# Value columns of two attention groups by seven block products, three units' weights prepared in the attention

## The chip, the cores and the metric

The kernel runs as one launch on one core of a Trainium2 chip. A core has engines that work side by side, each through its own instructions in their order: TensorE (PE, matrix products and, on a queue of its own, weight loads), VectorE (DVE), ScalarE (ACT), GpSimd (POOL) and SyncE (SP), which here starts nearly all transfers. They meet through semaphores. On-chip memory has 128 partitions; products are summed in 8 PSUM banks of 128 x 512 fp32. The metric is the device time of one execution in microseconds (us), lower is better.

## The reference, cut to what matters

The program is a two-layer decoder trunk over 1024 positions of width 1024 in fp32: layer 0 mixes positions with a chunked spatial gate, layer 1 is a dilated attention, each is followed by a squared-ReLU MLP of width 4096, and an RMS norm ends it. The change concerns the attention's products with `w_qkv`:

```python
qkv = (h @ w_qkv).astype(jnp.float32).reshape(B_, S_, 3, N_DIL_GROUPS, ATT_HEADS, HEAD_DIM)
...
for g, (window, dil) in enumerate(WINDOW_DILATIONS):
    n_, d_, m_ = _dilated_group(qkv[:, :, 0, g], qkv[:, :, 1, g], qkv[:, :, 2, g],
                                rb[:, g * ATT_HEADS:(g + 1) * ATT_HEADS], window, dil)
...
scales = [jnp.exp(m_ - m_all) for m_ in maxs]
num_sum = sum(n_ * c[..., None] for n_, c in zip(nums, scales))
den_sum = sum(d_ * c for d_, c in zip(dens, scales))
o = (num_sum / den_sum[..., None]).astype(h.dtype).reshape(B_, S_, ATT_WIDTH)
return o @ w_out
```

`h` here is normed. There are three groups of 8 heads of 64 columns with (window, dilation) = (128, 1), (512, 4), (2048, 16). In `_dilated_group` a query meets keys at the stride of its group, a bias from a table is added, and numerator, denominator and row maximum are returned. The values are 3 x 512 = 1536 columns, the queries and keys 3072.

## The kernel before, in words

**Products.** An fp32 operand is split into a rounded upper half and the rest (`split`: the copy to the upper half is on ACT at L219, the difference on DVE at L220). A product is three TensorE passes (upper x upper, upper x lower, lower x upper); one matmul instruction is a 128 x 128 weight against 128 x 512. Most large products also go by seven block products: two operands cut 2 x 2 need seven products of blocks and not eight, with sums of blocks formed before and of products after. All matmuls of this kind have line L191.

**Value stage** (`all_values`). The normed activations `y` lie in four blocks: half of the features x half of the positions. The 1536 value columns are three column groups `r` of 512. For each `r` and each half of the positions, 8 slices `k` of the features x 4 blocks of 128 positions x 3 passes are summed in four banks, directly and without block products: 96 matmuls. `firsts` holds the weights of column group 0; those of the next are loaded (`w_vt[r + 1, k]`, 256 KB each) and split in the second half of the current one, into the weight pool, which holds 8 pairs (tile name `wp`). Each finished bank is split into a tile `vs` and stored to `vd[r]` in DRAM.

Beside this run three generators. `terms_a.differences` forms, from the activations kept in fp32, the operands `t[4]` to `t[7]` of the block products for queries and keys; blocks 1 to 3 are `y` itself. `prepare` makes the seven weights of attention units 7, 8, 9 and 10: it loads four blocks of `w_qkv`, forms the sums on DVE, splits them (tiles `tr`) and stores both halves of each to `wd` in DRAM. `unit_weights`, advanced by `more()`, provides the weights of the units in their order: those of unit 0 are loaded, summed and split there, on POOL, the others are read back from `wd`, 512 KB each. Units 1 to 6 and 11 are prepared elsewhere, 11 by `prepare_apart`, which keeps the lower half in the tile that it loaded and puts the upper half in another, and hands the stores to `save`.

**Attention.** It has 12 units: 4 pairs of heads x 3 groups. `unit_qk` forms queries and keys of a unit by seven products (seven times 48 matmuls), reading `t[1]` to `t[7]` and the unit's weights. Other generators then form the scores (a DVE operation at L1401 adds the bias to the scores in PSUM and finds the maximum; ACT makes the exponentials at L1403), transpose them on TensorE (L198), split them (L219 and L220, tiles `tr`), multiply by the values `V`, which are loaded from `vd`, and merge the groups (tiles `N`; `od` in DRAM). A unit's bias is loaded (tile `t` from `bvec`) and copied by DVE, reversed, into a tile `b` at L1173 (`bias_turn`). The tag "b" of the pool `tpool` has two buffers, 128 x 512 each: the bias of unit i+1 goes into the one that unit i-1 leaves when its last scores are read.

**What sets the order.** TensorE's order is written by the program: a class `Flow` keeps a clock of estimated TensorE time, and the generators beside the main work yield a delay (the constants `PACE`, `LAT`, `CALM`, in ns) after which they are taken up again. On the other engines and in SP's queue the framework's scheduler orders the instructions by its own costs and priorities, and a pool's buffer is given again when its last reader has finished. SP starts the transfers in its order and waits there for what each needs.

## Time and profile before

| what | us |
|---|---|
| median of three runs (lowest to highest) | 2134.45 (2133.67 to 2135.84) |
| the profiled execution | 2131.01 |
| its span from first to last instruction | 2129.3 |
| one half (96 matmuls) of a value column group | 21.8 |
| unit 0 of the attention begins, from the span's start | 1059.6 |
| the attention's part that holds units 0 to 11, about | 1060 to 1396 |

One execution on the chip is recorded and shown as a page: the busy time of each engine, the same in 40 slices, the DMA queues, the chain of work that ended last (followed back from the end, at each step to what released it), the costliest groups of instructions and the DMA issues. The trace behind it answers closer questions: waits by what ended them, busy times by stretch of the span, a timeline. Times in rows are us, the mean of one instruction ns. A name as `wp<-r` is output and input tile, a line as L220 that of the code, where a helper's line stands for all that call it. "SPq" is SP's queue; a transfer's time is that from issue to landing.

### The profile page before, as it was taken

Reading aid. Unit: us, or ns where it says so; the run is one execution under the profiler, and the core shown is the slowest. Engines: PE = TensorE matmul, PEld = TensorE weight load, DVE = VectorE, ACT = ScalarE, POOL = GpSimd, SP = SyncE. Lnnn points to the kernel's source line nnn. Section 1 sums busy time; section 2 is a strip of 40 time slices with the busy share of each in tenths; the row PEclk is TensorE's granted clock in tenths of the full one; section 3 lists DMA queues with packets and bytes.
Section 4 is the critical chain, followed back from the end, with each engine's and each line's share of the span. In section 5 each row is a group of like instructions: output and inputs, shape, how many; then the busy total and the mean of one; then the engine's idle time right before and its main releaser. Section 6 shows DMA issues by size and latency. Waiting matters only on the chain.

```text
span 2129.3 us, 30657 instructions
## 1 busy us (share of the span) xinstructions
PE 2102.1 (99%) x10192; PEld 1739.0 (82%) x10192; DVE 1553.2 (73%) x2853; ACT 1170.5 (55%) x2360; POOL 511.1 (24%) x381
## 2 busy tenths in 40 slices
PE   9999999999999999999999999999999999999997
PEld 7888888888888888878888888887888888888886
DVE  7878769766789788688446666766985456987876
ACT  7645435566675444245356665766556556544432
POOL 2000224333324322420200000002343232433244
PEclk9999999999999999999999999999999999999999
DMA  6428814587756544449774656481256443654432
GB/s 218 125 92 287 289 59 139 202 284 270 265 195 201 163 144 139 139 173 323 267 231 148 182 157 177 164 275 61 74 200 210 152 155 125 207 163 153 149 114 79
DMA packets 221298, 380.79 MB, mean 179 GB/s; under 512 B 39513, under 2 KB 67284, under 8 KB 221140
## 3 DMA queue, kind: packets, MB, share of 16 engines
q1 hardware_dynamic: 212000, 377.48, 53.1%
q10 hardware_dynamic: 9140, 1.36, 0.4%
q8 instruction: 80, 1.31, 0.2%
q14 instruction: 78, 0.64, 0.1%
HBM read 245.94 MB, written 132.81 MB: 178 GB/s over the span
## 4 chain that ended last, share of the span: by engine, by line
PE 87%; DVE 6%; DMA 3%; ACT 1%; issue 1%; POOL 1%; SPq 0%; POOLq 0%; DVEq 0%; ACTq 0%
PE mm L191 44%; PE at L191 41%; PE at L198 2%; DVE y L220 1%; DVE t L220 1%; DVE wp L220 1%; DMA h<-in_xT 1%; DMA r<-in_w_v 0%; DVE r L437 0%; DMA t<-in_w_qkv 0%; DVE hx L220 0%; DMA V<-vd 0%; POOL t L277 0%; DVE h L332 0%; DVE b L442 0%
## 5 line engine op out<-in xcount | busy, mean ns | idle before, releaser
L219 ACT ACTIVATE wp<-r 128x512 fp32r<-128x512 f32 (+3 forms) x407 | 241.2, 597 | 352.1 <-PE at L191 217.2
L220 DVE TENSOR_TENSOR wp<-r,wp 128x512 fp32r<-128x512 f32 (+3 forms) x400 | 329.7, 829 | 132.8 <-ACT wp L219 130.0
L191 PE MATMUL mm<-t,wp 128*128 128x512 f32 x1368 | 345.4, 396 | 0.0
L191 PE MATMUL at<-hx,wp 128*128 128x512 f32 x1452 | 340.6, 389 | 1.5 <-DVE h L1043 1.5
L191 PEld LDWEIGHTS at<-hx,wp 128*128 128x128 f32 x1452 | 272.3, 188 | 59.1 <-DVE h L1043 2.4
L191 PEld LDWEIGHTS mm<-t,wp 128*128 128x128 f32 x1368 | 250.6, 188 | 52.6 <-issue 0.7
L277 POOL TENSOR_TENSOR t<-t 128x512 f32<-128x512 f32 (+1 forms) x64 | 82.2, 1284 | 686.5 <-ACT t L272 684.5
L191 PE MATMUL at<-y,wp 128*128 128x512 f32 x1008 | 245.3, 389 | 0.0
L191 PE MATMUL mm<-hx,wp 128*128 128x512 f32 x984 | 234.1, 389 | 0.0
L191 PEld LDWEIGHTS at<-y,wp 128*128 128x128 f32 x1008 | 189.1, 188 | 39.5 <-issue 0.3
L191 PEld LDWEIGHTS mm<-hx,wp 128*128 128x128 f32 x984 | 184.7, 188 | 38.3
L191 PE MATMUL mm<-y,wp 128*128 128x512 f32 x816 | 210.4, 397 | 1.2 <-DVE y L220 0.6
L375 POOL TENSOR_TENSOR t<-r 128x512 f32<-128x512 f32 (+3 forms) x62 | 82.9, 1336 | 480.2 <-DMA r<-in_w_up 136.9
L191 PEld LDWEIGHTS mm<-y,wp 128*128 128x128 f32 x816 | 149.1, 188 | 33.4 <-DVE y L220 1.0
L220 DVE TENSOR_TENSOR hx<-t,hx 128x512 fp32r<-128x512 f32 x192 | 162.6, 851 | 9.0 <-ACT hx L219 9.0
L191 PE MATMUL mm<-y,whi 128*128 128x512 f32 x512 | 158.2, 390 | 0.0
L219 ACT ACTIVATE hx<-t 128x512 fp32r<-128x512 f32 x192 | 119.1, 628 | 22.9 <-PE mm L191 10.0
L191 PE MATMUL at<-t,wp 128*128 128x512 f32 x552 | 130.6, 389 | 0.0
L377 POOL TENSOR_TENSOR r<-r 128x512 f32<-128x512 f32 (+3 forms) x62 | 91.0, 1468 | 163.5 <-DVE wp L220 156.5
L1043 DVE TENSOR_TENSOR h<-h,at 128x512 f32<-128x512 f32 x144 | 98.0, 681 | 34.9 <-PE at L191 34.2
L191 PEld LDWEIGHTS at<-t,wp 128*128 128x128 f32 x552 | 103.6, 188 | 21.5
L191 PEld LDWEIGHTS mm<-y,whi 128*128 128x128 f32 x512 | 95.6, 188 | 19.5
(228 smaller groups left out, 3452.4 us busy)
## 6 DMA issues: line engine op xcount, KB each, us to landing
t<-hid SPq DMA_DIRECT2D x182, 256.0 KB, 4.1
wd<-tr SPq DMA_DIRECT2D x154, 256.0 KB, 3.1
wp<-wd SPq DMA_DIRECT2D x77, 512.0 KB, 3.9
hid<-t SPq DMA_DIRECT2D x140, 256.0 KB, 2.9
r<-in_w_up SPq DMA_DIRECT2D x120, 256.0 KB, 2.8
r<-in_w_dn SPq DMA_DIRECT2D x80, 256.0 KB, 2.6
hid<-b SPq DMA_DIRECT2D x56, 256.0 KB, 2.9
r<-in_w_v SPq DMA_DIRECT2D x48, 256.0 KB, 3.1
```

The lines of the kernel that those rows point to most:

```text
L191: nc.tensor.matmul(out, lhsT, rhs, **kw)
L198: nc.tensor.transpose(out, src, ident)
L219: nc.scalar.activation(hi, src, AF.Copy)
L220: (engine or nc.vector).tensor_tensor(lo, src, hi.bitcast(F32), op=ALU.subtract)
L277: nc.gpsimd.tensor_tensor(self.acc, self.acc, sq, op=ALU.add)
L375: tt(r3, r[0, 0], r[1, 0], op=ALU.subtract)
L377: tt(r[1, 1], r[1, 0], r[0, 0], op=ALU.subtract)
L1043: return engine.tensor_tensor(hs[i, s], hs[i, s], src, op=ALU.add).ins
```

## The change

The value columns of group 0 stay as they are. Those of groups 1 and 2 together are now one 2 x 2 block product: features in two halves, and the two column groups. `VSEQ` is the order of the seven products; each takes 4 slices x 4 blocks x 3 passes for each of four position blocks at a time, 48 matmuls. The activation operands are the `t` that queries and keys use. The weight operands are made by `value_operands` as they are needed: it fetches `EARLY` operands ahead (32 loads of 256 KB for both groups, where there were 16), forms sums on DVE, 16 in all, and splits 28. Four banks `sums` collect products 1, 6, 7, 4, four others product 2 and then 5, 3. Tiles `uk` keep the copies (by ACT) that later sums need, and `added` makes the sum on DVE that `value_store` splits and stores. `differences` now forms its operands in the order in which these products need them.

With it the weights of the units move. Unit 7 is made in the value stage from product 6 on, by `prepare_apart`. Units 8, 9 and 10 are made in the attention: a generator is added there with a first delay of 12,000 and a `PACE` of 7,000 ns a step. Their loaded tiles `ra` have four buffers of the tag "r"; their upper halves `hi` lie in the tag "b", the two buffers of the bias tiles. Each unit has seven pairs: 21 `hi` in all, each split on ACT and DVE and stored with its `ra`. Unit 0's weights are formed on DVE and not on POOL. The bias of unit 0 is loaded in the value stage.

```diff
-PREPARED = ((1, 2, 3, 4, 5, 6), (7, 8, 9, 10))
+PREPARED = ((1, 2, 3, 4, 5, 6), (7,), (8, 9, 10))
 APART = 11
-PACE = (1700.0, 2500.0, 1900.0)
+EARLY = 4
+PACE = (1700.0, 1800.0, 3000.0, 7000.0)
...
         def differences(self, pace):
 
             tt = nc.vector.tensor_tensor
-            for k in range(4):
-                yield self.there[k], 0
-                (y00, y10), (y01, y11) = ((t[k][:, 0, :], t[k][:, 1, :]) for t in (self.kept, self.more))
-                for p, out, a, b in ((5, y00, y01, y00), (7, y01, y11, y01), (6, y11, y11, y00), (4, y10, y10, y11)):
-                    tt(out, a, b, op=ALU.subtract)
-                    self.t[p].append(pair(f"t{p}").split(out))
-                    yield pace
+            parts = [[t[k][:, j, :] for t in (self.kept, self.more) for j in range(2)] for k in range(4)]
+            for y00, y10, y01, y11 in parts:
+                tt(y00, y01, y00, op=ALU.subtract)
+                self.t[5].append(pair("t5").split(y00))
+                yield pace
+            for y00, y10, y01, y11 in parts:
+                tt(y01, y11, y01, op=ALU.subtract)
+                tt(y11, y11, y00, op=ALU.subtract)
+                self.t[6].append(pair("t6").split(y11))
+                yield pace
+                tt(y10, y10, y11, op=ALU.subtract)
+                self.t[7].append(pair("t7").split(y01))
+                yield pace
+            for y00, y10, y01, y11 in parts:
+                self.t[4].append(pair("t4").split(y10))
+                yield pace
...
-    def fetch(src):
-        r = rtemp()
+    def fetch(src, own=rtemp):
+        r = own()
         return r, load(src, r.bitcast(F32))
+
+    def apart():
+        return tpool.tile([P, HALF], F32R, tag="r", name="ra", bufs=4)
+
+    def above():
+        return tpool.tile([P, HALF], F32R, tag="b", name="hi", bufs=2)
...
-    def placed(dst, held):
+    def placed(dst, held, own=rtemp):
         lo, r = held
-        hi = rtemp()
+        hi = own()
         split(hi, lo, r)
         unsaved.extend((dst[:, e, :], t) for e, t in enumerate((hi, lo)))
...
-    def prepare_apart(i):
+    def prepare_apart(i, own=rtemp, upper=rtemp):
 
         tt = nc.vector.tensor_tensor
         n = 3 * (i // 3 * 3 + ORDER[i % 3])
         src = lambda a, b: w_qkv[n + a][:, half(b)]
-        put = lambda p, held: placed(wd[i, p], held)
-        r10, r11 = fetch(src(1, 0)), fetch(src(1, 1))
+        get = lambda a, b: fetch(src(a, b), own)
+        put = lambda p, held: placed(wd[i, p], held, upper)
+        r10, r11 = get(1, 0), get(1, 1)
...
+    def attended(unit_list, pace, *own):
+        for i in unit_list:
+            for _ in prepare_apart(i, *own):
+                yield pace
+                save()
+        save()
...
     def unit_weights():
 
-        tt = nc.gpsimd.tensor_tensor
+        tt = nc.vector.tensor_tensor
         for i, w in enumerate(unit_w):
...
             def put(p, src):
-                w[p] = wpair().split(src, nc.gpsimd)
+                w[p] = wpair().split(src)
...
+    def value_store(r, b, src):
+        v = slot((P, 4, 4, 64), F32R, "vs")
+        p4 = src.rearrange("p (u a c) -> p u a c", u=4, a=2)
+        hi, lo = v[:, :, 0:4:3, :], v[:, :, 1:3, :]
+        nc.scalar.activation(hi, p4, AF.Copy)
+        nc.vector.tensor_tensor(lo, p4, hi.bitcast(F32), op=ALU.subtract)
+        nc.sync.dma_start(vd[r][blk(b)], v.bitcast(F32))
+
+    VSEQ = (1, 2, 5, 6, 7, 3, 4)
+
+    def value_operands():
+        tt = nc.vector.tensor_tensor
+        parts = {1: ((1, 0),), 2: ((1, 4),), 5: ((2, 0), (2, 4)), 6: ((1, 0),), 7: ((2, 4),), 3: ((1, 4),), 4: ((2, 4),)}
+        order = [(p, k) for p in VSEQ for k in range(4)]
+        fetched = lambda p, k: [load(w_vt[a, b + k], raw() if p == 5 and not b else temp()) for a, b in parts[p]]
+        total, held = {}, [fetched(*x) for x in order[:EARLY]]
+        for n, (p, k) in enumerate(order):
+            r = held.pop(0)
+            if n + EARLY < len(order):
+                held.append(fetched(*order[n + EARLY]))
+            x = r[0]
+            if p == 5:
+                tt(x, r[0], r[1], op=ALU.add)
+                total[k] = x
+            elif p == 6:
+                x = total[k]
+                tt(x, x, r[0], op=ALU.subtract)
+            elif p in (7, 3):
+                tt(x, x, total[k], op=ALU.subtract)
+            yield wpair().split(x)
+
     def all_values():
 
...
+        operands, wv = value_operands(), []
+        for s in range(2):
+            ks = range(KT) if s == 0 else [4 * j + k for k in range(4) for j in range(2)]
+            banks = [mm_bank() if s == 0 and x < 3 else at_bank() for x in range(4)]
+            for n, k in enumerate(ks):
+                y = terms_a.blocks[k // 4, s]
+                flow.until(lambda: len(y) > k % 4)
                 for b, bank in enumerate(banks):
...
+                    x, w, c = y[k % 4], firsts[k], blk(b)
+                    matmul(bank, x.hi[:, c], w.hi, start=(k == 0), stop=False)
+                    matmul(bank, x.hi[:, c], w.lo, start=False, stop=False)
+                    matmul(bank, x.lo[:, c], w.hi, start=False, stop=(k == KT - 1))
+                    flow.pump()
+                if s:
+                    wv.append(next(operands))
+            for b, bank in enumerate(banks):
+                value_store(0, 4 * s + b, bank)
+        flow.add(terms_a.differences(PACE[1]))
+
+        uk = [slot((P, 2, HALF), F32, "uk") for _ in range(4)]
+
+        def added(x, bank):
+            t = temp()
+            nc.vector.tensor_tensor(t, x, bank, op=ALU.add)
+            return t
+
+        sums = None
+        for n, p in enumerate(VSEQ):
+            if p == 1:
+                sums = banks = [at_bank() for _ in range(4)]
+            elif p in (2, 5):
+                others = banks = [mm_bank() if b < 3 else at_bank() for b in range(4)]
+            else:
+                banks = others if p == 3 else sums
+            if p == 6:
+                flow.add(attended(PREPARED[1], PACE[2]))
+            opens = p in (1, 2, 5)
+            w = [wv.pop(0) for _ in range(4)]
+            x = terms_a.t[p]
+            for b, bank in enumerate(banks):
+                u, k1 = uk[b][:, 0, :], uk[b][:, 1, :]
+                for k in range(4):
+                    flow.until(lambda: len(x) > k)
+                    c, last = blk(b), k == 3
+                    matmul(bank, x[k].hi[:, c], w[k].hi, start=k == 0 and opens, stop=False, skip_group_check=True)
+                    matmul(bank, x[k].hi[:, c], w[k].lo, start=False, stop=False, skip_group_check=True)
+                    matmul(bank, x[k].lo[:, c], w[k].hi, start=False, stop=last, skip_group_check=True)
+                    flow.pump()
+                if p in (1, 6):
+                    nc.scalar.activation(u, bank, AF.Copy)
+                elif p == 2:
+                    value_store(1, b, added(u, bank))
+                elif p == 5:
+                    nc.scalar.activation(k1, bank, AF.Copy)
+                elif p == 7:
+                    value_store(2, 4 + b, added(k1, bank))
+                elif p == 3:
+                    value_store(1, 4 + b, added(u, bank))
+                else:
+                    value_store(2, b, bank)
+                if 0 < n < 6:
+                    wv.append(next(operands))
+                elif n == 6 and b:
+                    more()
+            if n == 5:
+                for _ in range(4):
+                    more()
+                U[0].rev = bias_tile(U[0].hp, U[0].g)
...
         if i == 0:
-            u.bias = bias_turn(*bias_tile(u.hp, g))
+            u.bias = bias_turn(*u.rev)
...
     all_values()
     for gen in (scorer, turner, valuer):
         flow.add(gen())
+    flow.add(attended(PREPARED[2], PACE[3], apart, above), 12000.0)
     for i in range(NU):
```

Where instructions stand now. On TensorE before, from the end of group 0's first half over its second half (the last 96 of the 99) into group 1, whose first half goes on as the last rows do (`wp` a weight pair, `y` a block of activations, `mm` and `at` banks of the two pools):

```order
L191 MATMUL mm<-wp,y 128x512 x9
L191 MATMUL at<-wp,y 128x512 x99
L191 MATMUL mm<-wp,y 128x512 x9
L191 MATMUL at<-wp,y 128x512 x3
L191 MATMUL mm<-wp,y 128x512 x9
```

The same place after (lines have moved by one): the second half of group 0 and product 1 (48 more), product 2 (48), then product 5 with the first four operands of `differences`:

```order
L192 MATMUL mm<-wp,y 128x512 x9
L192 MATMUL at<-wp,y 128x512 x147
L192 MATMUL mm<-wp,y 128x512 x36
L192 MATMUL at<-wp,y 128x512 x12
L192 MATMUL mm<-wp,t_9417 128x512 x3
L192 MATMUL mm<-wp,t_9430 128x512 x3
L192 MATMUL mm<-wp,t_9444 128x512 x3
L192 MATMUL mm<-wp,t_9458 128x512 x3
```

TensorE's order is 48 matmuls shorter. From unit 0 on it has the same shapes in both.

DVE before, from the bias copy for unit 4 to the row ahead of unit 4's first score read, an operation at L1401 (`N` the merge, `tr` transposed tiles, `q` and `k` lower halves of queries and keys, `st` a row's maxima):

```order
L1173 COPY b<-t 128x512
L1590 TENSOR_TENSOR N<-N,t 128x512
L1442 TENSOR_TENSOR N<-N,at 64x256
L1332 TENSOR_TENSOR t<-t,mm 128x512
L1442 TENSOR_TENSOR N<-N,at 64x256
L220 TENSOR_TENSOR tr<-at,tr 128x384
L1327 SCALAR_TENSOR_TENSOR q_11622<-t,q_11621 128x32x16
L220 TENSOR_TENSOR tr<-at,tr 128x384
L220 TENSOR_TENSOR tr<-N,tr 128x512
L1327 SCALAR_TENSOR_TENSOR k_11714<-mm,k_11713 128x32x16
L1442 TENSOR_TENSOR N<-N,at 64x256 x2
L220 TENSOR_TENSOR tr<-at,tr 128x384 x2
```

The same place after (the copy is now L1197, a split's difference L221, a score read L1494):

```order
L221 TENSOR_TENSOR ra<-ra,hi 128x512
L221 TENSOR_TENSOR tr<-at,tr 128x384
L221 TENSOR_TENSOR tr<-N,tr 128x512
L1420 SCALAR_TENSOR_TENSOR k_11724<-mm,k_11723 128x32x16
L221 TENSOR_TENSOR ra<-ra,hi 128x512
L1535 TENSOR_TENSOR N<-N,at 64x256 x2
L221 TENSOR_TENSOR ra<-ra,hi 128x512
L221 TENSOR_TENSOR tr<-at,tr 128x384 x2
L584 TENSOR_TENSOR ra<-ra 128x512
L1197 COPY b<-t 128x512
L1494 ISA t,st_11869<-at,b 128x128
L1494 ISA st_11869 128x1
```

The bias copy now stands directly ahead of the first scores that follow, behind splits whose `hi` use the buffer that the copy takes. Ahead of it in the whole gap stand four such splits; in the six gaps before units 2 to 7 there are three, four, three, four, three and four.

SP's queue at that place after (`wp<-wd` are weights of the coming units, `wd<-hi` and `wd<-ra` the stores of the new pairs, `ra<-in_w_qkv` their loads):

```order
L1390 DMA V<-vd_9037 64x4x256
L556 DMA wd_7_170<-hi 128x512
L556 DMA wd_7_170<-ra 128x512
L1241 DMA wp<-wd_4_146 128x1024
L556 DMA wd_3_173<-hi 128x512
L181 DMA ra<-in_w_qkv 128x512
L556 DMA wd_3_173<-ra 128x512
L1697 DMA od_1_11781<-tr 128x512
L556 DMA wd_6_171<-hi 128x512
```

The stores and loads of units 8 to 10, which stood in the value stage, are now among the attention's own transfers.

More of the change, by code (lines that the diff above doesn't have):

```diff
@@ L1246, in more @@
             next(ending, None)
-    def all_values():
-        ws, wn = firsts, []
-        for r in range(3):
-            if r == 1:
-                flow.add(prepare(PREPARED[1], PACE[2]))
-            for s in range(2):
-                ks = range(KT) if s == 0 else [4 * j + k for k in range(4) for j in range(2)]
-                banks = [mm_bank() if s == 0 and x < 3 else at_bank() for x in range(4)]
-                for n, k in enumerate(ks):
-                    y = terms_a.blocks[k // 4, s]
-                    flow.until(lambda: len(y) > k % 4)
-                    for b, bank in enumerate(banks):
-                        x, w, c = y[k % 4], ws[k], blk(b)
-                        matmul(bank, x.hi[:, c], w.hi, start=(k == 0), stop=False)
-                        matmul(bank, x.hi[:, c], w.lo, start=False, stop=False)
-                        matmul(bank, x.lo[:, c], w.hi, start=False, stop=(k == KT - 1))
-                        flow.pump()
-                    if s and r < 2:
-                        wn.append((k, wpair().split(load(w_vt[r + 1, k]))))
-                    elif s and n < AHEAD:
-                        more()
-                for b, bank in enumerate(banks):
-                    v = slot((P, 4, 4, 64), F32R, "vs")
-                    p4 = bank.rearrange("p (u a c) -> p u a c", u=4, a=2)
-                    hi, lo = v[:, :, 0:4:3, :], v[:, :, 1:3, :]
-                    nc.scalar.activation(hi, p4, AF.Copy)
-                    nc.vector.tensor_tensor(lo, p4, hi.bitcast(F32), op=ALU.subtract)
-                    nc.sync.dma_start(vd[r][blk(4 * s + b)], v.bitcast(F32))
-            if r == 0:
-                flow.add(terms_a.differences(PACE[1]))
-            ws, wn = dict(wn), []
```

10 lines of the change are left out of this document (5 added, 5 removed).

## The prediction

> **What bounds the kernel now.** I read the page's busy times first, then the chain that ended last, then TensorE's own waits, then busy times by stretch of the span, and last the timeline of the places that the change touches.
>
> ```profile
> span 2129.3 us, 30657 instructions
> PE 2102.1 (99%) x10192; PEld 1739.0 (82%) x10192; DVE 1553.2 (73%) x2853; ACT 1170.5 (55%) x2360; POOL 511.1 (24%) x381
> PE 87%; DVE 6%; DMA 3%; ACT 1%; issue 1%; POOL 1%; SPq 0%; POOLq 0%; DVEq 0%; ACTq 0%
> ```
>
> TensorE (PE) is busy for 99% of the span and makes up 87% of the chain. Its waits from the end of the value columns to the end of attention are these, as total, number and longest:
>
> ```profile
> PE at L191 <- DVE t L1574: 1.9, 3, 0.6
> PE mm L191 <- ACT o L219: 1.9, 1, 1.9
> PE mm L191 <- DVE h L332: 0.8, 1, 0.8
> PE at L191 <- DMA V<-vd: 0.7, 1, 0.7
> PE mm L191 <- DVE o L220: 0.2, 1, 0.2
> ```
>
> That is 5.5 us in 420. By stretches (all of the value stage but the first half of group 0; then attention):
>
> ```profile
> core 0: us, PE busy (x) PEld busy (x) DVE busy (x) ACT busy (x) POOL busy (x), PEclk, DMA share, GB/s
> 950.00:1060.00 110.00, 110.00 (x487) 91.13 (x486) 70.26 (x112) 49.07 (x87) 12.21 (x10) 1.00 0.81 295
> 1060.00:1396.00 336.00, 334.09 (x2081) 275.68 (x2079) 216.50 (x681) 213.49 (x590) 1.77 (x2) 1.00 0.59 176
> ```
>
> In the value stage PE never pauses, so a matmul less there is time saved, until another engine is late. VectorE (DVE) has 40 us free there. In attention PE pauses for 2 us in 336, and DVE and ScalarE (ACT) are busy for 64%.
>
> **What goes: 48 matmuls.** Groups 1 and 2 took 2 groups x 2 halves x 8 k x 4 blocks x 3 passes = 384; seven products take 7 x 4 x 4 x 3 = 336.
>
> ```profile
> 993.66 22.44 PE at L191 x99
> ```
>
> This piece of the chain gives 22.44 / 99 = 0.2267 us for one. 48 x 0.2267 = 10.9 us, all on PE. PE's order behind unit 0's start is the same, so nothing else of PE moves.
>
> **What the value stage gets.** Prices:
>
> ```profile
> L220 DVE TENSOR_TENSOR wp<-r,wp 128x512 fp32r<-128x512 f32 x8 | 5.5, 689 | 2.3 <-ACT wp L219 2.3
> L219 ACT ACTIVATE wp<-r 128x512 fp32r<-128x512 f32 x8 | 5.1, 632 | 5.5 <-PE at L191 5.3
> L220 POOL TENSOR_TENSOR wp<-r,wp 128x512 fp32r<-128x512 f32 x6 | 7.6, 1298 | 112.5 <-DMA vd<-vs 111.7 <-ACT wp L219 0.7
> r<-in_w_vt SPq DMA_DIRECT2D x8, 256.0 KB, 3.6
> ```
>
> DVE gains 51 operations in all: 12 more splits of value weights (28, not 16), 16 to form them, 12 sums with a kept product, and 11 of unit 0's weights that POOL did at 1.3 us each. It loses the 33 of units 8 to 10, which go to attention. In DVE's order 134 operations stand between the first stores of group 0 and unit 0's first q, where 115 stood. The 115 took the 70.26 us above, 0.61 each; 134 take 82 us, and PE's time there is 98. So DVE has room, if in order it is nowhere held up. The operand of a product can be split only when the product two before has released its weight buffer; walking the order with 0.61 us an operation, the tightest is the fourth operand of product 6, ready nearly 4 us ahead of PE. ACT gains 12 splits and 12 copies, loses 21 splits, and has 61 us free. The queue loses units 8 to 10 (18 loads and 42 stores of 256 KB) and gains 16 loads. I take 0 for the stage. Its bounds: not below 0, since PE waits for nothing there; above, one operand late by one load, 3.6 us.
>
> **What attention gets.** Units 8 to 10 bring 21 splits, 12 sums on DVE, 18 loads and 42 stores. As bare work, 33 x 0.61 = 20 us of DVE and 21 x 0.63 = 13 us of ACT go into some 190 us that have about a third free: nothing. What counts is where the upper halves lie: in the two buffers that hold the units' bias tiles. One is free only from the last score read of unit i-1 until the bias of unit i+1 is copied in. The order puts three or four upper halves into that gap in turn, six times (3, 4, 3, 4, 3, 4 for 21), and each has to be stored before the next is written. The copy waits for the last store, and behind it in DVE's order stand the score reads of unit i. The gap before unit 4 (four turns) now:
>
> ```profile
> 1196.03 0.42 DVE L1401 CUSTOM_DVE_ANT_0 t<-at,b 128x256 f32<-128x256 f32 x1
> 1198.06 0.42 DVE L1173 COPY b<-t 128x512 f32<-128x512 f32 x1
> 1205.98 1.02 DVE L220 TENSOR_TENSOR tr<-at,tr 128x384 fp32r<-128x384 f32 x2
> 1207.31 0.29 DVE L1401 CUSTOM_DVE_ANT_0 t<-at,b 128x128 f32<-128x128 f32 x1 [0.31 <-PE at L191]
> 1207.69 0.40 ACT L1403 ACTIVATE t<-t,st 128x128 f32<-128x128 f32 x1 [1.36 <-issue]
> 1208.87 0.39 ACT L1403 ACTIVATE t<-t,st 128x128 f32<-128x128 f32 x1
> 1211.08 1.03 PE L191 MATMUL at<-tr,V 128*128 128x256 f32 x8
> 1214.07 0.60 PE L198 MATMUL at<-ident,t 128*128 128x128 f32 x4
> ```
>
> The last read ends at 1196.45, and the copy, 1.6 us later, has 9 us to spare. The first read of unit 4 is at 1207.31, its exponentials end at 1209.26, and PE transposes them at 1214.07: 4.8 us in hand. The gap before unit 1 (three turns):
>
> ```profile
> 1100.95 0.08 DVE L1401 DVE_READ_ACCUMULATOR2_ANT st<- 128x1 f32 x1
> 1113.35 0.29 DVE L1401 CUSTOM_DVE_ANT_0 t<-at,b 128x128 f32<-128x128 f32 x1 [0.79 <-PE at L191]
> 1117.26 0.39 ACT L1403 ACTIVATE t<-t,st 128x128 f32<-128x128 f32 x1
> 1120.13 0.60 PE L198 MATMUL at<-ident,t 128*128 128x128 f32 x4
> ```
>
> 12.3 us, and 2.5 in hand at its eighth read. A turn is a split (0.63), two handovers (0.1 each, as from the read's end at 1207.60 to the exponential at 1207.69) and the store's landing. Landings, first attention, last the value stage:
>
> ```profile
> od<-tr SPq DMA_DIRECT2D x9, 256.0 KB, 2.9
> wp<-wd SPq DMA_DIRECT2D x67, 512.0 KB, 3.7
> V<-vd SPq DMA_DIRECT2D x12, 512.0 KB, 4.8
> wd<-tr SPq DMA_DIRECT2D x42, 256.0 KB, 3.3
> ```
>
> The nearest by size is 2.9, but the 60 added transfers are 15.7 MB in 190 us, 83 GB/s on 176, which takes the share from 0.59 to about 0.87 by its own ratio. That is the value stage's load, so I take 3.3: a turn is 4.13. Four turns, the copy (0.42) and the 1.95 from first read to last exponential: 16.5 + 2.4 = 18.9, so 1215.3 where PE needs 1214.07, 1.3 us late. Three times that is 4 us. Three turns with the copy take 12.8 for 12.3, inside the 2.5 in hand: 0. The ends: at 2.9 no passage costs anything; at 4.8 a four-turn one costs 7.3 and a three-turn one about 2.5, 29 us in all.
>
> By a rule of the Trainium skill (DMA: Bandwidth & Descriptors, on the anatomy of one DMA) a transfer takes 2.0 us and its bytes at 436 GB/s, an estimate of 2.6 us for 256 KB; by that the passages would cost nothing and the sum would be the first rival's. The same page (Latency and other measured facts) says that memory latency grows from 0.2 to 2 us under high load, which speaks against this change. The rows here, 2.9 at a share of 0.59 and 3.3 at 0.81, go that way.
>
> **The sum.** 2131.01 (profiled execution) - 10.9 + 0 + 4 = 2124.1. It stands 3.4 us under the median of the runs, so 2127.5 on their scale, 0.33% under 2134.45.
>
> **Rivals.**
> - *The whole saving stays* (landing about 2.9, or PE's slack is larger): 2134.45 - 10.9 = 2123.5. For it speaks the row of 256 KB stores in attention; against it the added load, and the order in which ACT does a split only behind other work.
> - *The passages eat most of the saving.* At 3.7, as 512 KB loads take, a turn is 4.53 and a four-turn passage 2.9 late, 8.6 in all: 2132.2, within 0.2%.
> - *VectorE holds the value stage.* If the operands of three products come late by one load each, 10.8 us go: 2138.3, also within 0.2%. Against it: 16 us free.
> - *Slower: the bias buffer decides.* At 4.3, between the loads' 3.7 and 4.8, a turn is 5.13: four turns 5.3 late, three turns 1 late, 19 us in all: 2142.5. It turns to slower by 0.2% where the stores land in 4.1 or more. For it speaks that V loads and weight loads stand just ahead of the stores in the one queue, which now waits for PE in front of them; a store behind such a wait lands later still:
>
> ```profile
> SPq L1217 <- PE mm L191: 167.5, 53, 5.4
> ```
>
> Against it: walking the six places, the load ahead of each first store is released in time. PE's waits would then pass 3 us. By the Trainium skill (TensorE: Matmul & The Clock Gate, Part 1) an idle window of some 3.4 us halves PE's clock, which would add to this rival; no run here shows it, with a clock of 1.00 in both stretches and no wait over 1.9.
>
> **Chances.** Forecast (2125.5 to 2130) 0.36; whole saving 0.22; passages at 3.7 0.13; VectorE 0.09; slower 0.20. A measurement of this kernel can tell about 0.2%, 4.3 us, from no change. Faster 0.58, same 0.22, slower 0.20. The range runs from 2122.5, the whole saving and 1 us of scatter, to 2141, which leaves out most of the slower case. The faster cases alone lie in 2123 to 2130.
>
> **What will show it.** The page should count 48 matmuls fewer (10144), and unit 0 should start about 98 us behind the second half of group 0, with no PE wait in between; a wait there for DVE or ACT at the weights means the third rival. DVE's count rises by 51. In attention I expect waits of 1 to 2 us before units 2, 4 and 6 for transposed tiles or exponentials, stores of the upper halves landing in about 3.3, and the bias copy idle on such a store. No waits there means the whole saving; waits of 5 us at all six places, the slower case. The prediction is wrong if the queue is blocked in attention so that weights of a unit come late, which I have at nothing.

## The result and the profile after

The changed kernel takes 2151.86 us (median of 6 runs, 2149.22 to 2156.07), the kernel before 2134.41 (6 runs). The ratio is 1.0081, with a 95% interval of 1.0068 to 1.0094: slower by 17 us, where 7 us less were forecast. The profiled execution has a span of 2149.0 us. Its page, in the lines that were shown of before:

```profile
span 2149.0 us, 30646 instructions
PE 2103.0 (98%) x10144; PEld 1736.4 (81%) x10144; DVE 1575.6 (73%) x2904; ACT 1183.9 (55%) x2384; POOL 498.0 (23%) x370
PE 79%; DVE 8%; DMA 6%; ACT 3%; issue 2%; POOL 1%; SPq 1%; ACTq 0%; DVEq 0%; POOLq 0%
```

TensorE has the 48 matmuls less, and yet its busy time is 0.9 us longer: the others took 11.8 us more. Its share of the chain fell from 87% to 79%, and DVE, DMA and ACT took what it lost. By stretches (the value stage from the same matmul as in the rows of before; then the attention), the longest of TensorE's waits from unit 0 on, and the chain in the value stage:

```profile
941.00:1051.00 110.00, 110.00 (x487) 91.10 (x486) 91.68 (x149) 57.39 (x100) 0.00 (x0) 1.00 0.58 210
1051.00:1410.00 359.00, 342.90 (x2072) 280.47 (x2070) 234.48 (x711) 222.95 (x607) 0.00 (x0) 0.98 0.66 205
```

```profile
PE at L192 <- DVE N L1535: 7.4, 5, 2.5
PE at L192 <- DVE tr L221: 3.6, 5, 1.7
PE at L192 <- DMA V<-vd: 2.6, 1, 2.6
```

```profile
1004.93 24.48 PE at L192 x108
1029.41 8.16 PE mm L192 x36
1037.57 13.60 PE at L192 x60
1051.17 8.84 PE mm L192 x39
```

The value stage runs without a pause, at 24.48 / 108 = 0.2267 us a matmul, and unit 0 starts at 1051.17 where it was 1059.6. In the attention TensorE is idle for 16 us of 359. As its order has the same shapes from unit 0 on, the two executions can be laid over each other matmul by matmul from the end. The shift of after against before is +2.4 us ahead of the value stage (waits at the program's start that change from execution to execution), -8.5 at unit 0 (so the stage gave 10.9), +15.8 from 1290 us of before on, when units 8 to 10 are made (24.3 lost in between), +19.4 behind the wait for `V` (3.6 more), and +19.7 at the end.

What happens in such a place, ACT and DVE ahead of unit 4's scores, then TensorE; the brackets give the idle time ahead and what ended it:

```profile
1209.02 0.63 ACT L220 ACTIVATE hi<-ra 128x512 fp32r<-128x512 f32 x1 [3.43 <-DMA wd<-hi]
1211.71 0.63 ACT L220 ACTIVATE hi<-ra 128x512 fp32r<-128x512 f32 x1 [0.61 <-DMA wd<-hi]
1218.08 0.40 ACT L1496 ACTIVATE t<-t,st 128x128 f32<-128x128 f32 x1 [4.97 <-DVE st L1494]
1217.41 0.43 DVE L1197 COPY b<-t 128x512 f32<-128x512 f32 x1 [2.25 <-DMA wd<-hi]
1213.71 0.88 PE L192 MATMUL at<-k,q 64*128 64x128 f32 x11 [1.70 <-DVE tr L221]
```

ACT stands at the third of the four upper halves (1209.02) until the second is stored, the bias copy stands behind the last store, and the first exponential comes at 1218.08. The chain of waits goes through three of the stores there (start, us); of its nine such pieces from 1090 to 1290 us four are longer than 5 us:

```profile
1203.78 5.16 DMA wd<-hi
1209.67 1.96 DMA wd<-hi
1212.37 4.96 DMA wd<-hi
```

### The profile page after: what moved, and what is told of

It reads as the page before. It is cut to its first block, busy times and chain, and to the rows that moved or that the text cites. A ratio compares the mean times of both kernels' runs of the same rounds, so it can differ in the third digit from the quotient of the medians.

```text
span 2149.0 us, 30646 instructions
## 1 busy us (share of the span) xinstructions
PE 2103.0 (98%) x10144; PEld 1736.4 (81%) x10144; DVE 1575.6 (73%) x2904; ACT 1183.9 (55%) x2384; POOL 498.0 (23%) x370
## 4 chain that ended last, share of the span: by engine, by line
PE 79%; DVE 8%; DMA 6%; ACT 3%; issue 2%; POOL 1%; SPq 1%; ACTq 0%; DVEq 0%; POOLq 0%
PE at L192 40%; PE mm L192 39%; DMA wd<-hi 2%; PE at L199 1%; DMA t<-in_w_qkv 1%; DVE tr L221 1%; DVE t L221 1%; DVE y L221 1%; POOL t L278 1%; DMA r<-in_w_v 1%; ACT t L1496 1%; DVE wp L221 1%; DMA V<-vd 0%; DVE r L438 0%; DVE h L333 0%
## 5 line engine op out<-in xcount | busy, mean ns | idle before, releaser
L221 DVE TENSOR_TENSOR wp<-r,wp 128x512 fp32r<-128x512 f32 (+3 forms) x399 | 322.8, 814 | 138.9 <-ACT wp L220 136.5
L220 ACT ACTIVATE wp<-r 128x512 fp32r<-128x512 f32 (+3 forms) x399 | 236.0, 596 | 328.4 <-PE at L192 202.5
L221 DVE TENSOR_TENSOR hx<-t,hx 128x512 fp32r<-128x512 f32 x192 | 162.1, 849 | 7.9 <-ACT hx L220 7.9
```

The lines of the kernel that those rows point to most:

```text
L220: nc.scalar.activation(hi, src, AF.Copy)
L221: (engine or nc.vector).tensor_tensor(lo, src, hi.bitcast(F32), op=ALU.subtract)
```

## The experiments

Times are medians of the same call's runs; the ratios are to the kernel before. "us" worked out from a ratio is that of 2134.4. Lines of code have moved with some edits, so that a helper has another number. A difference of two ratios carries about 0.2%, 4 us; one of 0.1% can't be told from nothing.

| run | median us | ratio, 95% interval |
|---|---|---|
| products, units 8 to 10 not made (none_made) | 2125.16 | 0.9958, 0.9943 to 0.9973 |
| units 8 to 10 moved, values direct (move_only) | 2158.82 | 1.0112, 1.0095 to 1.0129 |
| units 7 to 10 made in the value stage (in_value) | 2153.25 | 1.0088, 1.0073 to 1.0103 |
| upper halves in one own buffer (own_one) | 2152.67 | 1.0085, 1.007 to 1.01 |
| upper halves in tag t (among_t) | 2154.61 | 1.0106, 1.0086 to 1.0125 |
| lower half stored twice (unheld) | 2157.86 | 1.0109, 1.0094 to 1.0124 |
| their stores from ACT's queue (act_queue) | 2170.04 | 1.0167, 1.0149 to 1.0185 |
| 9500 ns a step (pace95) | 2150.98 | 1.0074, 1.0058 to 1.009 |
| operations alone (work_only) | 2142.07 | 1.0038, 1.0023 to 1.0052 |
| transfers alone (moves_only) | 2134.75 | 0.9995, 0.9985 to 1.0004 |
| operations alone, unit 8 only (work_one) | 2127.46 | 0.9967, 0.9955 to 0.9979 |
| operations alone, DVE's part on GpSimd (work_pool) | 2149.65 | 1.0062, 1.0043 to 1.008 |
| all, DVE's part on GpSimd (all_pool) | 2164.85 | 1.0138, 1.0118 to 1.0159 |
| ACT's operations alone (act_only) | 2127.57 | 0.9969, 0.9957 to 0.998 |
| DVE's operations alone (dve_only) | 2132.33 | 0.9991, 0.9983 to 1.0 |
| operations alone, upper halves in tag t (work_t) | 2128.23 | 0.9975, 0.9966 to 0.9984 |
| units 8 to 10 beside the first layer's down products (in_down) | 2128.61 | 0.9968, 0.9957 to 0.9979 |
| the same beside its up products (in_up) | 2175.07 | 1.0191, 1.0176 to 1.0206 |

**Which half of the change costs.** Theory A is the prediction's own: the bias buffers.

```diff
     # before, with the generators of after
+    flow.add(attended(PREPARED[2], PACE[3], apart, above), 12000.0)
```

> The kernel before with units 8 to 10 made in the attention as in the changed kernel (same tiles, same first delay and pace); the value columns stay direct. Theory A (each upper half holds a bias buffer until its store has landed; ACT, DVE and then TensorE stand behind it): the full loss of the attention, 24 us and up to 28 with the late V load: 2158 to 2163. Rival B (the 60 transfers and 54 operations cost by themselves, whatever buffer they use): the same here, told apart by the next two. Rival C (the block products cost in a place that is not in the value stage, by later V loads): nothing here, 2132 to 2139.

```diff
-    flow.add(attended(PREPARED[2], PACE[3], apart, above), 12000.0)
...
-                    nc.sync.dma_start(t.bitcast(F32), wd[i, p])
+                    nc.sync.dma_start(t.bitcast(F32), wd[i - 3 if i in PREPARED[2] else i, p])
```

> The changed kernel without the making of units 8 to 10: these units read the weights of units 5 to 7 again, so the same transfers come in for their weights, but 18 loads, 21 splits, 12 sums and 42 stores are left out, and the output is another. A and B: the products' saving alone, 2134.4 - 10.9 = 2123.5, with up to 2 us for a late V load. C: no saving, 2134 or more.

The move alone costs 24 us, the products alone gain 0.42%, 9 us. So the loss lies in making units 8 to 10 in the attention: 0.81% + 0.42% = 1.23%, 26 us. Theory C falls but for a rest: the last wait for `V` is there in none_made too (2.4 us, 0.7 before and in move_only). Laid over before, none_made loses 3.3 us there and nothing else in the attention. The longest of these loads landed in 11.0 to 11.7 us in six executions with the products (9.7 in moves_only), in 8.9 and 9.3 before and in move_only. Why is open.

**Back in the value stage.**

```diff
-            if p == 6:
-                flow.add(attended(PREPARED[1], PACE[2]))
+            if p == 2:
+                flow.add(prepare((7, 8, 9, 10), 1900.0))
```

> The changed kernel with units 7 to 10 made in the value stage from product 2 on, in the way and at the pace (1900 ns) of the kernel before; the attention gets nothing. A: the attention's loss goes; DVE gets back 33 operations of 0.61 us, 20 us, in a stage where it had 16 free, so it comes 0 to 10 us late there, as TensorE's waits for DVE in the value stage or the first units: 2123 to 2134. B: 2123 too. If VectorE or the queue holds the value stage harder (loads 42 more stores), over 2136.

It loses as much as the changed kernel does. TensorE waits in the value stage and at the first weights, SP's queue stands at the stores of this work, and ACT stands at loads of the value operands:

```profile
PE at L192 <- ACT wp L220: 9.8, 5, 4.7
PE mm L192 <- DMA wp<-wd: 4.3, 1, 4.3
SPq L517 <- ACT tr L220: 15.5, 11, 3.8
ACT wp L220 <- DMA t<-in_w_vt: 7.0, 4, 2.8
```

So taking this work out of the stage was needed for the products to run without a pause, and VectorE's free time was not the only measure there.

**The buffers of the upper halves.**

```diff
-        return tpool.tile([P, HALF], F32R, tag="b", name="hi", bufs=2)
+        return tpool.tile([P, HALF], F32R, tag="u", name="hi", bufs=1)   # own_one
+        return tpool.tile([P, HALF], F32R, tag="t", name="hi")   # among_t
...
+        unsaved.extend((dst[:, e, :], t) for e, t in enumerate((lo if own is above else hi, lo)))   # unheld
```

> The changed kernel with the upper halves of units 8 to 10 in one buffer of their own, so that the bias copies wait for none of them; two upper halves still can't be in flight at once, but they may come at any time, seven for one bias copy and not three or four inside a gap. A: the loss falls to what is left of ACT's waits for the one buffer, 0 to 8 us: 2123 to 2132. B: the operations and transfers are all there, so 2148 to 2154 as the changed kernel.

> The changed kernel with the upper halves of units 8 to 10 among the 13 buffers of the tag t: no bias copy and no later upper half waits for the store of an earlier one. Theory A2 (what holds is the one free buffer, as the row of own buffers suggests: ACT stands in its order at the next upper half until the store of the last one has landed, and queries, exponentials and merges stand behind it): the loss falls under 10 us, 2124 to 2134. Rival B (the splits, sums and transfers cost by themselves, or by SP's queue, which waits for each): 2146 to 2154, no change.

> The changed kernel with the same tiles, but the lower half of units 8 to 10 is stored in both places, so that the output is another: all transfers and operations are there, and an upper half is only held until VectorE has made the lower half from it. A2: 2124 to 2134 as with the buffers of tag t. B by the splits and transfers: 2146 to 2154.

None of the three gains anything: A falls in the form that was forecast, in which freeing the bias buffer takes the loss away. Own_one loses 24.7 us of its 26.1 ahead of the scores of units 1 and 2: without the bias buffers the work comes earlier, its upper halves between 1065 and 1176 us, where after has them from 1093 to 1280. In among_t no bias copy and no upper half waits for a store any more, but other operations of the same work do. These are DVE's and SP's waits in it, 1060 to 1300 us (the profiled execution is the fastest of four, 2145.2 us):

```profile
DVE ra L596 <- DMA ra<-in_w_qkv: 10.9, 3, 7.9
DVE ra L600 <- DMA ra<-in_w_qkv: 5.8, 2, 3.5
DVE ra L590 <- DMA wd<-ra: 3.3, 1, 3.3
SPq L181 <- DMA wd<-ra: 37.9, 14, 6.1
```

The sums of blocks now stand in DVE's order until the next block is loaded, and that load waits in SP's queue until a store has freed one of the four `ra` buffers. In after such waits were 22.5 us at upper halves and bias copies, and about 5 at loads (same stretch, some of the rows):

```profile
DVE b L1197 <- DMA wd<-hi: 6.3, 3, 3.4
DVE b L1197 <- DMA wd<-ra: 1.6, 1, 1.6
ACT hi L220 <- DMA wd<-hi: 14.6, 6, 3.4
DVE ra L584 <- DMA ra<-in_w_qkv: 2.2, 2, 1.8
```

Freed buffers let the work run faster up to the next transfer; the waiting moves, the loss stays.

**Queue and pace.**

```diff
+        unsaved.extend((dst[:, e, :], t, nc.scalar if own is above and e == 0 else nc.sync) for ...)   # act_queue
...
-PACE = (1700.0, 1800.0, 3000.0, 7000.0)
+PACE = (1700.0, 1800.0, 3000.0, 9500.0)   # pace95
```

> The changed kernel with the stores of the upper halves of units 8 to 10 started by ACT behind its own split and not by SP: SP's queue doesn't wait for them any more (36 us of its waits), and nothing of SP's stands ahead of them. If SP's place makes the landing long: the loss falls by a third or more, 2132 to 2144. If it is the buffer and a landing that stays at 2 to 5 us: 2146 to 2153.

> The changed kernel with 9500 ns a step for units 8 to 10 where it has 7000: two or three upper halves in a gap (2, 3, 2, 3, 3, 2, 3, 3), not three or four. A and A2: the gaps with two cost nothing, those with three some 3 to 4 us: 2138 to 2147. B: the same work later, 2148 to 2154.

From ACT's queue the stores cost 18 us more. ACT starts them itself, and its waits for a store at an upper half rise from 14.6 to 20.6 us; what makes the rest is not shown. Fewer upper halves in a gap change nothing that can be told (1.0074 against 1.0081). The loss is not one of a fourth turn alone.

**Operations or transfers.** Theory A3: ACT and DVE stand, in their order, at side work that waits for a transfer. B: the operations crowd the engines. D: the transfers hold up the queue.

```diff
+            if not resident:
+                resident.extend(fetch(src(0, 0), own) for _ in range(4))
+            get = lambda a, b: next(around)
+            put = lambda p, held: split(upper(), *held)   # work_only
...
+        put = lambda p, held: unsaved.extend((wd[i, p][:, e, :], held[0]) for e in range(2))   # moves_only
```

> The changed kernel with the 21 splits and 12 sums of units 8 to 10 at their places and in the same buffers, but on four tiles that lie there: all their loads but four and all their stores are left out, and these units read the weights of units 5 to 7, so the output is another. Theory A3 (ACT and VectorE stand in their order at operations of this side work that wait for a transfer: a store's landing, a bias copy behind it, or a load that waits for a buffer; the attention's own operations stand behind them): no transfer to stand at, so the products' saving is left, 2123 to 2129. Rival B (the splits and sums themselves crowd the two engines): 2142 to 2152. Rival D (the transfers hold up SP's queue and the attention's own loads): 2123 to 2129 as A3, told apart by the next.

> The changed kernel with the 18 loads and 42 stores of units 8 to 10 at the same pace and in the same four buffers, without the splits and sums: what was loaded is stored twice, no upper half is made, and the output is another. A3: ACT and VectorE have nothing to stand at, so 2123 to 2131. B: the same. D: the loss stays, 2142 to 2152, with TensorE's waits at weights or values that come late.

Against none_made the operations alone cost 0.80%, 17 us, so A3 doesn't explain the loss by itself. The transfers alone cost 0.37%, 8 us, but in another place than any loss of the changed kernel. With no upper half made they come earlier than the edit intends: the stores start between 1072 and 1155 us, in after between 1094 and 1281. The loss is one place. ACT starts the transfers of the row statistics (`sc`) itself. By the trace's semaphore events each start stands until the last transfer on the semaphore that it uses has landed: the first until 1131.52, for a load of weights (`wp<-wd`), the second until 1132.14, for a load of this work. Behind them stand the queries of the next unit:

```profile
1131.59 1.28 ACTq L1636 DMA_DIRECT2D sc<-st  x2
1132.92 0.63 ACT L1446 ACTIVATE q<-t 128x512 fp32r<-128x512 f32 x1 [9.01 <-DMA ra<-in_w_qkv]
```

TensorE's wait for those keys is 6.3 us, and its granted clock is 0.86 over these 50 us, as it is half for 13.7 us from 1135 on:

```profile
PE mm L192 <- DVE k L1447: 6.3, 1, 6.3
1100.00:1150.00 50.00, 43.66 (x245) 35.30 (x243) 18.84 (x70) 21.27 (x70) 0.00 (x0) 0.86 0.97 291
```

In after the same queries stand for 1.5 us, until a DVE operation is done; no start of ACT's waits for a load there:

```profile
1124.77 0.63 ACT L1419 ACTIVATE q<-t 128x512 fp32r<-128x512 f32 x1 [1.52 <-DVE t L1425]
```

So this run shows that such a load of the queue can cost, and not what the transfers cost in the changed kernel. That 17 and 8 add up to nearly the 26 proves nothing. D as I meant it was not seen either: no weight came late.

**Why 33 operations cost 17 us.** DVE was busy for 64% of the attention, but not evenly. Four stretches of before: around unit 2's first scores, ahead of unit 3's, ahead of unit 4's and behind the first of these (DVE stands behind PE and PEld):

```profile
1131.00:1148.00 17.00, 17.00 (x105) 13.87 (x104) 8.81 (x34) 9.09 (x29) 0.00 (x0) 1.00 0.59 165
1160.00:1176.00 16.00, 16.00 (x109) 13.34 (x108) 13.99 (x50) 12.44 (x34) 0.00 (x0) 1.00 0.49 149
1190.00:1206.00 16.00, 15.36 (x94) 12.84 (x93) 14.76 (x31) 11.27 (x27) 0.00 (x0) 1.00 0.57 165
1206.00:1220.00 14.00, 14.00 (x93) 11.18 (x92) 5.91 (x31) 8.27 (x32) 0.00 (x0) 1.00 0.88 232
```

DVE is busy for 52, 87, 92 and 42% of them. Theory E is that the operations cost where DVE is dense; F that ACT is the late engine.

```diff
+            put = lambda p, held: split(upper(), *held, nc.gpsimd)   # work_pool, with the sums on GpSimd too
...
+    flow.add(attended(PREPARED[2][:1], PACE[3], apart, above), 12000.0)   # work_one
```

> As the run with the operations alone (units 8 to 10 on four resident tiles, no transfers), but the 21 differences and 12 sums are on GpSimd, which does 1.8 us of work in this stage; the 21 copies stay on ACT. Theory E (the operations cost where VectorE has no free time: it is busy for 87 and 92% between units, 1160 to 1176 and 1190 to 1206 us before the change, though for 64% over the stage): the 17 us fall under 7, 2125 to 2132. Rival F (ACT is the engine that is late, or any operation put into the chain costs, wherever): 2136 to 2143.

> The changed kernel, all work in it, with the differences and sums of units 8 to 10 on GpSimd. E: the operations' 17 us go but for a few, the transfers' 9 to 10 us stay, and so does what the engines wait for them: 2133 to 2142. F: 2148 to 2154.

> The operations alone, for unit 8 and not for 9 and 10: 7 splits and 4 sums, in two gaps. E: a third of the 17 us or less, since the first gap of the changed kernel cost nothing: 2125 to 2131. If the loss were one of the code as a whole and not of the places, 2136 or more.

Unit 8 alone costs 0.09%, 2 us, which can't be told from nothing. GpSimd made it worse, with a difference of 1.29 us for DVE's 0.69, and both runs with it came out above what E and F gave. ACT then waits for it at the one free bias buffer, so they don't part E from F:

```profile
ACT hi L220 <- POOL ra L221: 9.1, 12, 1.4
```

The last three take the engines apart, and the buffer (upper copies alone; 33 DVE operations on resident tiles alone; both, with the upper halves in tag t):

```diff
+            put = lambda p, held: nc.scalar.activation(upper(), held[1], AF.Copy)   # act_only; no sums
...
+            put = lambda p, held: tt(held[0], held[1], resident[...][1], op=ALU.subtract)   # dve_only
...
-        return tpool.tile([P, HALF], F32R, tag="b", name="hi", bufs=2)
+        return tpool.tile([P, HALF], F32R, tag="t", name="hi")   # work_t
```

> As the run with the operations alone, but only ACT's part: the 21 copies to an upper half, without the 33 operations of VectorE; units 8 to 10 read the weights of units 5 to 7. Theory E (VectorE's dense stretches between units): no loss but 0 to 4 us, 2124 to 2129. Rival F (ACT is late, at 0.63 us a copy ahead of queries, keys and exponentials): 10 us or more of the 17, 2134 to 2142. If it takes both (a chain that goes from ACT to VectorE and back), 2127 to 2134 here and in the next.

> The other part alone: 33 operations on VectorE at the same places (21 differences of resident tiles, 12 sums), without the copies on ACT. E: 10 us or more of the 17, 2134 to 2142. F: 2124 to 2129.

> The operations alone on both engines, with the upper halves among the 13 buffers of the tag t and not in those of the bias tiles. If the order of turns in one buffer (ACT's next copy behind VectorE's difference) or the bias copies behind them cost some of the 17 us, that part goes: under 2138. If the buffers cost nothing without a transfer: 2139 to 2146.

Against none_made ACT's part costs 0.11% (2 us), DVE's 0.33% (7 us), and both with free buffers 0.17% (4 us). ACT's copies stood where work_only has them, so F falls: ACT alone is not late. DVE's did not: with no upper half made all 33 stand between 1070 and 1107 us, and 8.5 us are lost ahead of unit 1's scores. That run says that the operations cost when they are crowded together, and nothing of DVE's part of the 17 us.

So the bias buffers make most of the 17 us, 13, where no transfer holds them. They do it by the order. The bias copy must come behind the last upper half in its buffer, and the scores behind the copy, so three or four splits stand ahead of the scores in the dense stretch. Rows of DVE in work_only, then at the same place in work_t (others left out):

```profile
1193.77 1.17 DVE L1434 SCALAR_TENSOR_TENSOR k<-t,k 128x512 fp32r<-128x512 f32 x1
1195.44 0.69 DVE L221 TENSOR_TENSOR ra<-ra,hi 128x512 fp32r<-128x512 f32 x1
1196.97 0.67 DVE L221 TENSOR_TENSOR ra<-ra,hi 128x512 fp32r<-128x512 f32 x1
1199.07 0.68 DVE L221 TENSOR_TENSOR ra<-ra,hi 128x512 fp32r<-128x512 f32 x1
1200.87 0.69 DVE L221 TENSOR_TENSOR ra<-ra,hi 128x512 fp32r<-128x512 f32 x1
1204.31 0.42 DVE L1211 COPY b<-t 128x512 f32<-128x512 f32 x1
```

```profile
1189.37 1.16 DVE L1434 SCALAR_TENSOR_TENSOR k<-t,k 128x512 fp32r<-128x512 f32 x1
1191.04 0.42 DVE L1211 COPY b<-t 128x512 f32<-128x512 f32 x1
1200.26 0.68 DVE L221 TENSOR_TENSOR ra<-ra,hi 128x512 fp32r<-128x512 f32 x1
```

With free buffers the copy stands 1.7 us behind the keys and one split ahead of the scores; with the bias buffers it is 10.5 us and four.

Where the loss lies is seen when the profiled executions are laid over before, as above. Each column is what TensorE loses in the gap ahead of that unit's scores, in us (the six gaps are those before units 1 to 6; the bias copies in them are for units 2 to 7):

| run | 1 | 2 | 3 | 4 | 5 | 6 | sum |
|---|---|---|---|---|---|---|---|
| after | 0.3 | 5.4 | 4.7 | 4.3 | 2.9 | 6.7 | 24.2 |
| operations alone (work_only) | 1.3 | 0.7 | 3.8 | 3.9 | 0.2 | 5.5 | 15.3 |
| the same, free buffers (work_t) | 0.5 | 0.1 | 0.6 | 1.4 | 1.2 | 0.0 | 3.7 |
| transfers alone (moves_only) | 0.0 | 11.9 | 0.0 | 0.0 | 0.0 | 0.0 | 11.8 |

Ahead of units 3, 4 and 6 the operations alone make 13.1 of the 15.7 us that after loses. DVE was dense there before: 87, 92 and (1256 to 1272 us) 82%. Ahead of units 2 and 5, where it was busy for 52 and (1220 to 1240 us) 54%, they make 0.9 of 8.3. The rest comes with the transfers: in these two gaps the chain of after goes through four stores of upper halves, of 3.2 to 5.5 us. This fits E gap by gap; no run changes how dense DVE is at one place and nothing else.

**A better place.**

```diff
-    flow.add(attended(PREPARED[2], PACE[3], apart, above), 12000.0)
...
+        if layer == 0:
+            flow.add(attended(PREPARED[2], PACE[3]))
         down.run(w)   # in_down
...
-LATER = (2, 4, 6)
+LATER = (1, 2, 3, 4, 5, 6)   # in_up, with units 8 to 10 ahead of 11 in that chain
```

> The changed kernel with units 8 to 10 made beside the first layer's down products (700 to 900 us of the span, where the DMA share is 0.41 to 0.49 and VectorE is busy for 81%), in the tag t and at 7000 ns a step; the attention gets nothing. By A3 it depends on what stands behind these waits there: VectorE has 35 us free and gets 20; if the stretch has slack, the products' saving stays, 2123 to 2128, otherwise up to 10 us are lost, 2134.

> The same with units 8 to 10 made beside the first layer's up products (400 to 600 us, VectorE busy for 68%, DMA share 0.75), where unit 11 is made already, in 24 more of the steps there. Where the loaded queue decides, 2128 to 2140; where VectorE's free time decides, 2123 to 2128.

Beside the down products all of this work costs 0.10%, 2 us, and the kernel is faster than both: 2128.61 us, 0.32% under before (0.21 to 0.43). DVE is at 172.5 of 200 us there, from 154.5 before (77%, where 81 were expected), and TensorE never pauses; one wait near 641 us, where the work begins, is 3.2 us long where it was 0.9. Beside the up products, at a DMA share of 0.75 before (400 to 600 us), TensorE's busy time falls to 85.8 of 100 us; its chain there goes through loads of weights (tr) of 3 to 5 us. First in_down, then in_up:

```profile
700.00:900.00 200.00, 200.00 (x884) 165.58 (x884) 172.53 (x236) 96.73 (x170) 71.69 (x54) 1.00 0.63 202
```

```profile
400.00:500.00 100.00, 85.80 (x345) 68.04 (x344) 62.23 (x77) 56.16 (x98) 23.96 (x16) 0.92 0.84 289
```

## Why the prediction was wrong

The stores of the upper halves in after, with the median from issue to landing:

```profile
wd<-hi SPq DMA_DIRECT2D x21, 256.0 KB, 2.6
```

- **The products' 10.9 us: right.** Unit 0's shift gives 10.9, and the products alone gained 9 us with an interval of 6 to 12. That "nothing else of PE moves" was wrong: the late `V` takes back 3.3 us in the trace of none_made.
- **0 for the value stage: right**, with no wait of TensorE. DVE took 79.7 us of the last 98 where the working had 82.
- **"As bare work ... go into some 190 us that have about a third free: nothing": this step failed.** The operations alone cost 17 us, 15.3 of them in the attention's trace, where the changed kernel loses 24.2. With free buffers they cost 4, so it is not their number but the place that the bias buffers force on them, a cost for which the sum has no term. The third free was a mean over stretches from 42 to 92%, and three of the six gaps end in dense ones.
- **+4 for the passages through the bias buffers: the place was right, the sum mis-sized.** It priced these buffers by the landing of a store alone, with 3.3 us. The 21 stores landed in 2.6 by the median (the row above), from 2.0 to 5.5. By the working a landing of 2.9 or less costs nothing, and three turns cost nothing at 3.3. Measured, the gaps of three turns (ahead of units 1, 3 and 5) lost 7.9 us, those of four (2, 4 and 6) 16.3. So a usual landing is not what the buffers cost; beside the order it is, by the chain, the slow stores: four of its nine over 5 us. That the 24.2 us come near the 29 which the working gave for landings of 4.8 is chance.
- **The queue "blocked in attention" so that weights come late, at nothing: right for the changed kernel.** TensorE waits for no weight there. The transfers alone, which came earlier, cost 8 us by two starts of ACT's.
- **The rival that ended slower came nearest**, with the right place and a chance of 0.20, but not by its mechanism. It asked for landings of 4.3 and for waits of TensorE past 3 us, up to 5 in all six gaps; the longest there was 2.5, and the loss without any store was not in it. Its price of 19 us also lacked the half-rate clock and the late `V`.

## What to carry to other kernels

A share of busy time over a stage does not say that added work is free: look at the stretch where the work will stand in an engine that takes its instructions in order, and at what its buffer forces it ahead of. Side work that alternates with transfers through few buffers makes each engine wait at whichever operation meets the transfer, so freeing one buffer moves the wait; move the work to a stretch whose engines are not on the path (here the down products, for 2 us). Try the two halves of a change apart before mending either: the products alone were a gain all the time. And when a run leaves something out, look where the rest then stands, before its time is read as the price of a part: here two such runs had moved the work that they were to price.

## What the runs showed of the hardware

TensorE's granted clock fell to half after short waits. These windows of after are at 1141 and 1281 us, the waits those in the 6 us ahead of the first:

```profile
1137.00:1141.00 4.00, 1.89 (x15) 1.50 (x16) 2.66 (x11) 2.53 (x10) 0.00 (x0) 1.00 0.92 285
1141.10:1144.50 3.40, 3.31 (x10) 2.34 (x9) 1.12 (x4) 0.87 (x3) 0.00 (x0) 0.50 0.98 293
1281.00:1287.80 6.80, 6.08 (x28) 5.41 (x29) 4.19 (x20) 5.33 (x20) 0.00 (x0) 0.50 0.63 216
```

```profile
PE at L192 <- DVE st L1494: 1.2, 1, 1.2
PE at L192 <- DVE N L1535: 1.2, 1, 1.2
```

Four such windows, of 3.4, 3.4, 6.8 and 3.4 us, hold 17.0 us between 1141 and 1431; at half rate that is up to 8.5 us of the 27.9 that the attention and the late `V` lost, beside the waits themselves. The Trainium skill (TensorE: Matmul & The Clock Gate, Part 1) gives half rate after an idle window of about 3.4 us. The windows' length agrees; here two waits of 1.2 us, with TensorE busy for 1.89 of the 4 us ahead, or one of 2.3 to 2.6, were enough. Single waits of 1.7 us (at 1213.71) and 1.9 us (at 1483) left the clock at 1.00. In the prediction this stood as an addition to a rival that no run had shown; it is up to 30% of that loss. The execution before shows half rate too, outside the stretches looked at there: behind a wait of 2.4 us its granted clock is 0.53 from 2118 to 2129 us.
